# Layer 0's down-projection in three passes that mix context with halves of the latent blocks, and norm statistics by one product with a full matrix of 1/D

## The chip, the cores and the metric

The kernel runs on one core of a Trainium2 chip. The metric is the device time of one execution in microseconds (us); the time before is the median of three runs. The engines are PE (TensorE, matmuls), DVE (VectorE), ACT (ScalarE), POOL (GpSimd) and SP (SyncE), whose queue issues nearly all DMA transfers.

## The reference, cut to what matters

A diffusion transformer of two layers: 1024 latent tokens and 256 context tokens, width D = 1024. Each layer has a token mixer (differential attention in layer 0, neighbourhood attention in layer 1) and then a gated feed-forward network (FFN) of inner width 2816 with a short convolution over the positions. Latent and context share weights and are modulated by different vectors; layer 1 needs no context after its mixer.

```python
def rmsnorm(t, g):
    tf = tf * lax.rsqrt(jnp.mean(tf * tf, axis=-1, keepdims=True) + NORM_EPS)
    return tf * g
def conv_ffn(t, w_up, w_conv, b_conv, w_down):
    ...                                            # up-projection, depthwise conv of 3 taps
    return (jax.nn.silu(g) * a) @ w_down           # (n, 2816) @ (2816, 1024)
# in every layer, after the mixer:
    h2 = rmsnorm(x, norm_ffn[i]) * (1.0 + sc2) + sh2
    x = x + g2 * conv_ffn(h2, ...)
    if need_ctx:                                   # layer 0 alone
        xc = xc + cg2 * conv_ffn(hc2, ...)
```

The case is about the last product, `@ w_down`, and about the `mean` of the norm.

## The kernel before

**Layout and passes.** Activations lie with the features on the 128 partitions and the tokens along the free axis. There are three blocks of tokens: 0 and 1 (latent, 512 tokens each) and 2 (context, 256). The down-projection has 22 chunks k of the inner width and 8 chunks j of 128 output features. Every product runs as three matmuls of a high and a low part (high x high, high x low, low x high), so a block costs 22 x 8 x 3 = 528 matmuls of 512 columns, or 256 for the context. Layer 0 makes one pass for each block, in the order 2, 0, 1 (`ORDER`); layer 1 one for block 0 and one for block 1. A pass keeps its sums in eight PSUM banks, six from one pool and two from another. It takes k = 0 and 1 for six of the j, then k = 2, then the other two j, then k = 3 to 18 with all j, and at the end the last three k with j outside, so that the sums end one after the other; `end(j)` then combines a sum with x on DVE (L780), stores it (L782, layer 0) and adds its square to the norm's sums SS (L375 on ACT, L376 on DVE). For the context, x is loaded again just before that (L779), each into one of seven small buffers `t`; for blocks 0 and 1, x lies in a tile X that is loaded during the pass.

**The weights.** Each pass fetches all of `down` again: 22 tiles of 128x1024 (512 KB, L128), made into a high part on ACT (L138) and a low part on POOL (L142) in a ring `wsp` of five tiles, up to four ahead of PE.

**The activations g.** `load_g` brings the FFN's inner activations from DRAM into `t` (L758) and makes the high part on ACT (L555) and the low part on DVE (L556; the first four of a layer on POOL). They lie in two buffers of four k each, T1 and T2, used in turn and freed as a whole: a pass's first g can be written when the pass before has read its last g of that buffer.

**Work beside it in layer 0.** `hook0` adds work for layer 1. In pass 1 (block 0), after each k = 3 to 18, one of 16 quarters of layer 1's modulation weights is loaded into the one buffer `ug` (512 KB, L1238) and multiplied into `rows` by four DVE operations (L1244, L1246). At the start of pass 2 `ada_columns` (`turn`) turns `rows` into columns by 64 small matmuls (L1254) and frees the place where block 1's X goes. In pass 2 (block 1), after every other k = 3 to 17, a pair of up-projection tiles of layer 1 is loaded through the weights' raw buffers (two of four), added in four POOL operations (L182 to L185) and stored (two times 512 KB).

**The norm.** `rnorm_steps` makes 1/rms of a block for all partitions: for each 128 tokens a matmul of SS by a 128x2 matrix of 1/D (L388), which gives a column per 128 tokens; Sqrt (L391) and reciprocal (L392) of the columns; DVE spreads the columns on a diagonal (L394); a product with a matrix of ones brings them to all partitions (L398), and ACT copies the result to R (L399). The second product stands one section of PE's program later, where the generator is taken up again. The kernel calls it 13 times, 10 for 512 tokens and 3 for 256. In pass 2 of layer 0 it is called for block 0, whose norm for layer 1 (`write0`, 16 DVE operations, L412 and L414) follows there.

**The order.** PE's order in the FFN is that of the code (`manual(engines={pe})`); the other engines' orders are set by the scheduler. An engine's queue is served in order: what stands behind a waiting instruction waits too.

Of the kernel before, what the change touches and what calls it, by code (L numbers as in the profile page):

```python
# [52 lines left out]
ADA_AT = [(1, k) for k in range(3, 19)]  # L53
SUM_AT = [(2, k) for k in range(3, 19, 2)]
# [150 lines left out]
def _body(nc, tc, es, a, out):  # L205
# [58 lines left out]
    mean_w = const.tile([P, 2], F32, name="mean_w")  # L264
    V.memset(mean_w, 1.0 / D)
    ones = const.tile([P, P], F32, name="ones")
    V.memset(ones, 1.0)
    rcol, rn_count = const.tile([P, 2, 4], F32, name="rcol"), [0]
# [70 lines left out]
    def ada_dve(l, n, yp, pool, tag=None):  # L339
# [38 lines left out]
    def rnorm(*args):  # L378
        for R in rnorm_steps(*args):
            pass  # L380
        return R

    def rnorm_steps(yp, pool, SS, b0, n):

        nt = n // P
        ps = yp.tile([P, 512], F32, name="rn_ps", tag="y")
        for t in range(nt):
            T.matmul(out=ps[:, 2 * t:2 * t + 2], lhsT=SS[:, b0 + t * P:b0 + t * P + P], rhs=mean_w, start=True, stop=True)  # L388
        col = rcol[:, rn_count[0] % 2]
# [155 lines left out]
    def ffn(l, X, H, SS, np_, hp, hp2, xpool, yp, bp, hook=None, write=None, turn=None):  # L545
# [89 lines left out]
        with manual(engines={pe}):  # L635
            late, steps = [], None
            for i in range(NF if l == 0 else ne):
# [26 lines left out]
                if i == 1:  # L664
                    chain = rnorm_steps(yp, np_, SS, 512, 512)
                    next(chain)
                if i == 2:
                    R.append(next(chain))
                    steps = token_forms()
# [982 lines left out]
```

## Time and profile before

| | us |
|---|---|
| time, median of 3 runs | 3296.74 (3295.65 to 3296.87) |
| the profiled execution | 3302.75 |
| its span, first to last instruction | 3301.0 |
| PE busy | 3139.8 (95%) |
| DVE busy | 2141.8 (65%) |
| ACT busy | 1397.1 (42%) |
| POOL busy | 1750.4 (53%) |

The mean granted clock of PE is 0.971 of full speed. Layer 0's down-projection lies at 1566 to 1944 us of the span, that of layer 1 at 3036 to 3285. A stretch of the span is read by its busy times, by the count of its instructions in brackets, and by its granted clock (PEclk, 1.00 is full speed). An instruction's idle time in square brackets is that of its engine just before it, with the work that ended it.

### The profile page before, as it was taken

The page shows a single profiled execution, that of the slowest core. Times are in us where ns is not written, and L with a number is a line of the kernel's source. Part 1 is how long each engine was busy: PE and PEld are TensorE (multiplying, and loading weights), DVE is VectorE, ACT ScalarE, POOL GpSimd, SP SyncE. Part 2 cuts the span into 40 slices and gives each one's busy share as a digit, 9 for nine tenths or more (in the row PEclk, how much of TensorE's full clock was granted, in tenths as well). Part 3 has the DMA queues.
Part 4 walks back from the last instruction along what each step waited for, and adds up shares of the span by engine and source line. Part 5 has one row for each costly group of instructions (what it writes and reads, how often), then busy time and mean ns, then how long its engine had stood idle before and what let it go on. Part 6 is the DMA issues. An engine that isn't in the chain of part 4 may idle for free.

```text
span 3301.0 us, 43509 instructions
## 1 busy us (share of the span) xinstructions
PE 3139.8 (95%) x15632; PEld 2597.7 (79%) x15632; DVE 2141.8 (65%) x3294; ACT 1397.1 (42%) x2388; POOL 1750.4 (53%) x984
## 2 busy tenths in 40 slices
PE   8999889999899999999899989999999999999998
PEld 4888767777588888888777768888898778887876
DVE  6577488888547677777665554315995667776253
ACT  3221167777224454444332232225994444443111
POOL 2214166666227876777643752113663277777763
PEclk9999999999799999999998999999999999999999
DMA  7565334332525744344764667736884334334541
GB/s 265 158 205 185 121 104 119 105 111 70 191 95 193 232 159 141 131 144 154 237 219 172 216 234 252 244 131 167 194 206 145 100 126 144 130 122 159 199 166 58
DMA packets 248456, 536.82 MB, mean 163 GB/s; under 512 B 28976, under 2 KB 101552, under 8 KB 248240
## 3 DMA queue, kind: packets, MB, share of 16 engines
q1 hardware_dynamic: 247232, 533.71, 50.9%
q8 instruction: 124, 2.03, 0.3%
q14 instruction: 92, 0.75, 0.1%
q10 hardware_dynamic: 1008, 0.32, 0.0%
HBM read 395.24 MB, written 138.67 MB: 162 GB/s over the span
## 4 chain that ended last, share of the span: by engine, by line
PE 65%; DVE 11%; POOL 9%; issue 7%; DMA 5%; ACT 3%; SPq 0%; ACTq 0%; POOLq 0%; DVEq 0%
PE w_ps L609 21%; PE qk_ps L429 10%; PE w_ps L771 7%; POOL wsp L142 4%; PE wo_ps L429 3%; PE o L1048 3%; PE sl L997 2%; PE v_ps L440 2%; PE o L1438 2%; PE v_ps L439 2%; PE v_ps L441 2%; PE tp L1024 2%; PE w_ps L429 2%; DVE E L999 1%; POOL wf L150 1%
## 5 line engine op out<-in xcount | busy, mean ns | idle before, releaser
L142 POOL TENSOR_TENSOR wsp<-raw,wsp 128x1024 fp32r<-128x1024 f32 (+2 forms) x285 | 666.2, 2345 | 669.2 <-ACT wsp L138 570.4
L771 PE MATMUL w_ps<-g,wsp 128*128 128x512 f32 (+1 forms) x2640 | 568.6, 377 | 40.7 <-POOL wsp L142 14.6
L771 PEld LDWEIGHTS w_ps<-g,wsp 128*128 128x128 f32 x2640 | 471.4, 193 | 136.5 <-POOL wsp L142 17.8
L429 PE MATMUL qk_ps<-Hh,wsp 128*128 128x512 f32 x1280 | 319.7, 372 | 0.0
L140 POOL TENSOR_SCALAR wsp<-raw 128x1024 fp32r<-128x1024 f32 x72 | 100.2, 1393 | 391.9 <-DMA raw<-in_wqk_dram 150.0
L609 PE MATMUL w_ps<-FT,wf 128*128 128x512 f32 x1200 | 290.8, 394 | 12.2 <-ACT wf L149 5.8
L138 ACT CAST wsp<-raw 128x1024 fp32r<-128x1024 f32 (+1 forms) x213 | 193.8, 926 | 237.3 <-DMA raw<-in_down_dram 71.1
L609 PEld LDWEIGHTS w_ps<-FT,wf 128*128 128x128 f32 x1200 | 226.3, 189 | 64.9 <-POOL wf L150 6.6
L556 DVE TENSOR_TENSOR g<-t,g 128x512 fp32r<-128x512 f32 (+1 forms) x102 | 144.2, 1459 | 185.7 <-ACT g L555 183.1
L429 PEld LDWEIGHTS qk_ps<-Hh,wsp 128*128 128x128 f32 x1280 | 215.3, 188 | 38.2
L609 PE MATMUL w_ps<-FT,wsp 128*128 128x512 f32 x912 | 214.0, 390 | 0.0
L1004 ACT ACTIVATE E<-E,st 128x1280 f32<-128x1280 f32 x128 | 175.3, 1369 | 66.2 <-DVE st L999 65.1
L609 PEld LDWEIGHTS w_ps<-FT,wsp 128*128 128x128 f32 x912 | 171.1, 188 | 36.7 <-DVE t L700 0.2
L1014 POOL TENSOR_TENSOR E<-E,E 128x1280 f32<-128x1280 f32 x64 | 188.5, 2946 | 5.3
L1012 POOL TENSOR_SCALAR E<-E,st 128x1280 f32<-128x1280 f32 x64 | 85.9, 1342 | 191.9 <-DVE st L1007 103.4
L999 DVE CUSTOM_DVE_ANT_0 E<-sl,zero,st 128x1024 f32<-128x1024 f32 x128 | 163.7, 1280 | 21.4 <-PE sl L997 20.7
L429 PE MATMUL qk_ps<-Hl,wsp 128*128 128x512 f32 (+1 forms) x640 | 175.3, 371 | 0.0
L609 PE MATMUL w_ps<-Hh,wsp 128*128 128x512 f32 x528 | 173.7, 394 | 0.9 <-ACT p L621 0.9
L997 PE MATMUL sl<-kst,q 128*128 128x512 f32 x512 | 158.7, 433 | 1.6 <-DVE st L999 1.6
L353 DVE SCALAR_TENSOR_TENSOR ada<-raw,c_cvec,ada 128x512 f32<-128x512 f32 x168 | 135.5, 840 | 36.7 <-DMA raw<-in_ada_w_dram 35.4
L1048 PE MATMUL o<-T,vt 128*128 128x512 f32 (+1 forms) x464 | 154.2, 460 | 0.6 <-ACT ot L1055 0.5
L1375 POOL TENSOR_SCALAR E<-E,st 128x640 f32<-128x640 f32 (+1 forms) x128 | 99.5, 778 | 83.5 <-DVE st L1374 69.0
(608 smaller groups left out, 7024.1 us busy)
## 6 DMA issues: line engine op xcount, KB each, us to landing
raw<-in_down_dram SPq DMA_DIRECT2D x110, 512.0 KB
raw<-in_ada_w_dram SPq DMA_DIRECT2D x80, 512.0 KB
gscr<-work SPq DMA_DIRECT2D x44, 512.0 KB
t<-gscr SPq DMA_DIRECT2D x88, 256.0 KB
raw<-sscr SPq DMA_DIRECT2D x38, 512.0 KB
raw<-in_up_dram SPq DMA_DIRECT2D x33, 512.0 KB
raw<-in_wqk_dram SPq DMA_DIRECT2D x32, 512.0 KB
q<-qscr SPq DMA_DIRECT2D x256, 64.0 KB
```

Source lines behind the costliest of these rows:

```text
L138: nc.scalar.copy(out=sp[:, 0, c:c + n], in_=raw[:, c:c + n])
L142: nc.gpsimd.tensor_tensor(out=sp[:, 1, c:c + n], in0=raw[:, c:c + n], in1=f32(sp[:, 0, c:c + n]), op=ALU.subtract)
L353: stt(out=accs[v], in0=tv[:, kk, :], scalar=scol[:, kc, v:v + 1], in1=accs[v], op0=ALU.mult, op1=ALU.add)
L429: T.matmul(out=ps, lhsT=w[:, kc, :], rhs=H[b][s][:, kc, :], start=(kc == 0 and i == 0), stop=(kc == KC - 1 and i == 2))
L556: eng.tensor_tensor(out=form[:, kc, 1, :], in0=x, in1=f32(form[:, kc, 0, :]), op=ALU.subtract)
L609: T.matmul(out=ps, lhsT=w, rhs=form(kc, s), start=(start and kc + i == 0), stop=(kc == 3 and i == 2), skip_group_check=not start)
L771: T.matmul(out=ys[j][:, :n], lhsT=w[:, j, :], rhs=g[:, k % 4, s, :], start=(k == 0 and i == 0), stop=(k == NF - 1 and i == 2))
L997: T.matmul(out=ps[:, 512 * c:512 * c + 512], lhsT=qs[2 * j + s][:, qc], rhs=ks[j][:, 512 * c:512 * c + 512], start=(s == 0), stop=(s == 1))
L999: V.tensor_tensor_reduce(out=E[j][:, :SEQ], in0=ps, in1=zero.broadcast_to([P, SEQ]), op0=ALU.add, op1=ALU.min, scale=-1.0, scalar=m, accum ...
L1004: S.activation(out=E[j], in_=E[j], func=AF.Exp, scale=-1.0, bias=m, accum_out=sm)
L1014: G.tensor_tensor(out=E[0], in0=E[0], in1=E[1], op=ALU.add)
L1048: T.matmul(out=o[:, :n], lhsT=w, rhs=x, start=(i == 0 and j == 0), stop=(i == len(seq) - 1 and j == len(three) - 1))
```

## The change

**Passes.** `PASSES` gives each pass a list of segments (block, its j). Layer 0: pass 0 has the whole context and j = 0 to 3 of block 0; pass 1 has j = 4 to 7 of block 0 and j = 0 to 3 of block 1; pass 2 has j = 4 to 7 of block 1 and fetches only the right half of each weight tile (128x512). Two context sums share one PSUM bank. Layer 1 keeps its two passes. The count of matmuls is the same; the weight tiles of layer 0 become 44 whole and 22 half ones in place of 66, the g tiles 88 of 512 columns and 22 of 256 in place of 44 and 22.

**g.** Each of the two buffers is one ring whose slots are used again one by one. With two segments each has its ring, four k deep; with one segment both make a ring of eight. `load_g(at, k)` loads up to four (five) k ahead, over the end of the pass.

**Work beside it.** The modulation quarters move to pass 0, the sums of up weights to pass 1, `turn` stays at pass 1 (now the mixed pass), block 0's norm is made in pass 2 as before. A mixed pass keeps the last two k for the end, not three.

**Norm.** `rnorm` makes one product of a 128x128 matrix of 1/D with SS (128x512), which gives the mean on all partitions at once; Sqrt and reciprocal then work on 128x512, and there is no generator.

```diff
+ALL, LOW, HIGH = range(KC), range(4), range(4, KC)
+PASSES = ((((2, ALL), (0, LOW)), ((0, HIGH), (1, LOW)), ((1, HIGH),)), (((0, ALL),), ((1, ALL),)))
-ADA_AT = [(1, k) for k in range(3, 19)]
-SUM_AT = [(2, k) for k in range(3, 19, 2)]
+ADA_AT = [(0, k) for k in range(3, 19)]
+SUM_AT = [(1, k) for k in range(3, 19, 2)]
...
-    mean_w = const.tile([P, 2], F32, name="mean_w")
+    mean_w = const.tile([P, P], F32, name="mean_w")
...
-    def rnorm_steps(yp, pool, SS, b0, n):
...
+    def rnorm(yp, pool, SS, b0, n):
+        ps = yp.tile([P, 512], F32, name="rn_ps", tag="y")
+        T.matmul(out=ps[:, :n], lhsT=mean_w, rhs=SS[:, b0:b0 + n], start=True, stop=True)
+        R = pool.tile([P, 512], F32, name="R", bufs=rbufs[0])
+        S.activation(out=R[:, :n], in_=ps[:, :n], func=AF.Sqrt, bias=eps)
+        V.reciprocal(out=R[:, :n], in_=R[:, :n])
         return R
...
+        rings = hp2.tile([P, 4, 2, 512], F32R, name="g0", tag="T2"), hp.tile([P, 4, 2, 512], F32R, name="g1", tag="T1")
+        def slot(at, i, k):
+            q = at * NF + k
+            r = i if len(passes[at]) > 1 else q // 4 % 2
+            return rings[r][:, q % 4, :, :BLOCKS[passes[at][i][0]][1]].unsqueeze(1)
...
+            last = at * NF + k + (4 if len(passes[at]) > 1 else 5)
+            while loads and loads[0][0] * NF + loads[0][1] <= last:
...
+                        if b == 2 and j % 2:
+                            ys[i, j] = ys[i, j - 1][0], CTX
...
+                done = at > 0 and all(b for b, _ in segs)
+                if done:
+                    R.append(rnorm(yp, np_, SS, 0, 512))
...
+                if done:
+                    write(0, out_[0], R[-1])
...
+                n_last = 2 if len(segs) > 1 else 3
...
+                    load_g(at, k - 1)
...
+                    if item[1] < 2:
+                        end(item)
+                    elif x % 2:
+                        end(sums[x - 1])
+                        end(item)
...
+        for segs in PASSES[l]:
+            j0 = min(js[0] for _, js in segs)
             for k in range(NF):
-                W.add(a["down"][l, k])
+                W.add(a["down"][l, k][:, P * j0:])
```

**The order, first place: SP at the boundary between layer 0's passes 0 and 1.** `t<-xspill` loads x of one context chunk, `xscr<-t` stores its result, `xscr<-X` stores one of block 0, `raw` is a weight tile, `t<-gscr` a tile of g. Before:

```order
L782 DMA xscr<-t 128x256
L779 DMA t<-xspill_125 128x256
L128 DMA raw_14547<-in_down_dram 128x1024
L782 DMA xscr<-t 128x256
L779 DMA t<-xspill_125 128x256
L128 DMA raw_14597<-in_down_dram 128x1024
L128 DMA raw_14637<-in_down_dram 128x1024
L782 DMA xscr<-t 128x256
```

Now:

```order
L781 DMA xscr<-t 128x256
L778 DMA t<-xspill_124 128x256
L781 DMA xscr<-t 128x256
L778 DMA t<-xspill_124 128x256
L781 DMA xscr<-X_13805 128x512 x3
L781 DMA xscr<-t 128x256
L778 DMA t<-xspill_124 128x256
L781 DMA xscr<-X_13805 128x512
```

Three stores of block 0's ends now stand ahead of the load of x for the fifth context chunk; loads and stores of the context still take turns.

**Second place: DVE where the modulation rows are made.** `rows<-ug` is the work of L1246 (now L1253), four for a quarter, `g<-t,g` a low part of g. Before, in the block 0 pass:

```order
L1246 SCALAR_TENSOR_TENSOR rows<-ug,c_cvec,rows 128x512 x11
L556 TENSOR_TENSOR g_14995<-t,g_14995 128x512 x2
L1246 SCALAR_TENSOR_TENSOR rows<-ug,c_cvec,rows 128x512
L556 TENSOR_TENSOR g_14995<-t,g_14995 128x512 x2
L1244 TENSOR_SCALAR rows<-ug,c_cvec 128x512 x2
L1246 SCALAR_TENSOR_TENSOR rows<-ug,c_cvec,rows 128x512 x10
```

Now, in pass 0:

```order
L542 TENSOR_TENSOR g_13638<-t,g_13638 128x256
L1253 SCALAR_TENSOR_TENSOR rows<-ug,c_cvec,rows 128x512 x4
L542 TENSOR_TENSOR g_13639<-t,g_13639 128x512
L542 TENSOR_TENSOR g_13638<-t,g_13638 128x256
L1253 SCALAR_TENSOR_TENSOR rows<-ug,c_cvec,rows 128x512 x4
L542 TENSOR_TENSOR g_13639<-t,g_13639 128x512
```

One quarter now stands between the g of one k and that of the next.

**Third place: DVE at block 0's norm in layer 0's last pass.** L412 and L414 (now L398 and L400) are the norm's scaling and low part. Before:

```order
L392 RECIPROCAL rcol<-rcol 128x4
L394 TENSOR_TENSOR R<-c_ident,rcol 128x512
L556 TENSOR_TENSOR g_15384<-t,g_15384 128x512
L412 SCALAR_TENSOR_TENSOR X_14594<-X_14594,scale_1_93,R 128x512 x3
L414 SCALAR_TENSOR_TENSOR Hl_15509<-X_14594,mod_91,Hh_15508 128x512 x3
L412 SCALAR_TENSOR_TENSOR X_14594<-X_14594,scale_1_93,R 128x512 x4
L414 SCALAR_TENSOR_TENSOR Hl_15509<-X_14594,mod_91,Hh_15508 128x512 x4
L412 SCALAR_TENSOR_TENSOR X_14594<-X_14594,scale_1_93,R 128x512
L556 TENSOR_TENSOR g_15640<-t,g_15640 128x512 x2
```

Now:

```order
L385 RECIPROCAL R<-R 128x512
L542 TENSOR_TENSOR g_13638<-t,g_13638 128x512
L398 SCALAR_TENSOR_TENSOR X_13805<-X_13805,scale_1_92,R 128x512 x3
L400 SCALAR_TENSOR_TENSOR Hl_15968<-X_13805,mod_90,Hh_15967 128x512 x3
L398 SCALAR_TENSOR_TENSOR X_13805<-X_13805,scale_1_92,R 128x512 x4
L400 SCALAR_TENSOR_TENSOR Hl_15968<-X_13805,mod_90,Hh_15967 128x512 x4
L398 SCALAR_TENSOR_TENSOR X_13805<-X_13805,scale_1_92,R 128x512
L542 TENSOR_TENSOR g_13638<-t,g_13638 128x512 x2
```

The sequence is the same; the reciprocal is 128 times as wide for each partition, the spreading on the diagonal is gone, and the pass around it has four sums for each k in place of eight.

## Rows read from the trace of the kernel before

**Rows 1.** The page: span and engines (busy us, share of the span, instructions)
```profile
span 3301.0 us, 43509 instructions
...
PE 3139.8 (95%) x15632; PEld 2597.7 (79%) x15632; DVE 2141.8 (65%) x3294; ACT 1397.1 (42%) x2388; POOL 1750.4 (53%) x984
```

**Rows 2.** Six stretches of layer 0's down-projection; columns as named in the first line
```profile
core 0: us, PE busy (x) PEld busy (x) DVE busy (x) ACT busy (x) POOL busy (x), PEclk, DMA share, GB/s
1566.33:1640.65 74.32, 66.86 (x529) 65.24 (x527) 50.68 (x35) 29.51 (x42) 56.60 (x25) 0.95 0.72 239
1640.65:1674.61 33.96, 17.36 (x64) 13.11 (x63) 22.43 (x32) 7.40 (x13) 8.55 (x3) 0.80 0.56 174
1674.61:1796.83 122.22, 118.12 (x501) 95.92 (x502) 78.36 (x83) 42.79 (x57) 56.78 (x22) 0.97 0.63 216
1796.83:1809.00 12.17, 12.17 (x70) 12.17 (x68) 1.07 (x8) 0.00 (x0) 0.00 (x0) 0.60 0.00 1
1809.00:1881.30 72.30, 72.30 (x309) 58.88 (x309) 38.38 (x27) 22.13 (x30) 48.30 (x26) 0.97 0.61 221
1881.30:1944.42 63.12, 51.22 (x191) 39.63 (x191) 18.02 (x17) 15.19 (x21) 44.25 (x26) 0.86 0.74 259
```

**Rows 3.** Undisturbed context matmuls, then layer 1's two down passes; columns as in rows 2
```profile
1592.00:1602.00 10.00, 10.00 (x88) 10.00 (x87) 10.00 (x5) 4.07 (x6) 10.00 (x5) 1.00 0.74 232
3036.12:3156.20 120.08, 120.08 (x531) 99.27 (x529) 45.05 (x39) 19.34 (x31) 83.69 (x46) 1.00 0.55 185
3156.20:3284.60 128.40, 125.48 (x538) 102.50 (x537) 56.67 (x48) 23.44 (x39) 73.99 (x39) 0.97 0.36 119
```

**Rows 4.** PE in time, context pass to block 0: start, us, work [idle, releaser]
```profile
1649.41 0.79 PE L771 MATMUL w_ps<-g,wsp 128*128 128x512 f32 x1 [8.76 <-ACT g L555]
1655.33 8.73 PE L771 MATMUL w_ps<-g,wsp 128*128 128x512 f32 x29 [5.13 <-DVE g L556]
```

**Rows 5.** DVE in time, same boundary: first and last of the eight context ends
```profile
1637.49 0.47 DVE L780 SCALAR_TENSOR_TENSOR t<-w_ps,mod,t 128x256 f32<-128x256 f32 x1
...
1674.08 0.48 DVE L780 SCALAR_TENSOR_TENSOR t<-w_ps,mod,t 128x256 f32<-128x256 f32 x1
```

**Rows 6.** Modulation rows on DVE, 1698.76 to 1759.74 us: totals, then two quarters in time
```profile
L1246 DVE SCALAR_TENSOR_TENSOR rows<-ug,c_cvec,rows 128x512 f32<-128x512 f32 x28 | 24.8, 942 | 21.1 <-DMA ug<-in_ada_w_dram 21.1
...
L1244 DVE TENSOR_SCALAR rows<-ug,c_cvec 128x512 f32<-128x512 f32 x4 | 4.0, 1021 | 4.4 <-DMA ug<-in_ada_w_dram 4.3
...
1719.04 2.74 DVE L1246 SCALAR_TENSOR_TENSOR rows<-ug,c_cvec,rows 128x512 f32<-128x512 f32 x4 [2.91 <-DMA ug<-in_ada_w_dram]
1725.37 2.74 DVE L1246 SCALAR_TENSOR_TENSOR rows<-ug,c_cvec,rows 128x512 f32<-128x512 f32 x4 [3.58 <-DMA ug<-in_ada_w_dram]
```

**Rows 7.** The up-weight sums' first add on POOL: first and last of eight
```profile
L182 POOL TENSOR_TENSOR raw253g<-raw253g x1: 1738/1738/1738, 1829.1 to 1829.1; 128x512 f32<-128x512 f32 x1
...
L182 POOL TENSOR_TENSOR raw267g<-raw267g x1: 1277/1277/1277, 1929.3 to 1929.3; 128x512 f32<-128x512 f32 x1
```

**Rows 8.** Norm statistics and reciprocals, grouped by line and shape, whole span
```profile
L388 PE MATMUL rn_ps<-mean_w,SS 128*128 128x2 f32 x92 | 15.0, 283 | 11.1 <-DVE SS L376 11.1
...
L392 DVE RECIPROCAL rcol<-rcol 128x4 f32<-128x4 f32 x10 | 1.7, 174 | 11.6 <-ACT rcol L391 11.6
...
L1210 DVE RECIPROCAL m_all<-m_all 128x32 f32<-128x32 f32 x2 | 0.7, 352 | 0.8 <-ACT m_all L1209 0.8
```

**Rows 9.** DVE and POOL in time during block 0's norm in the block 1 pass
```profile
1821.13 10.26 DVE L412 SCALAR_TENSOR_TENSOR X<-X,scale,R 128x512 f32<-128x512 f32 x4
...
1821.00 8.15 POOL L142 TENSOR_TENSOR wsp<-raw,wsp 128x1024 fp32r<-128x1024 f32 x3 [32.03 <-ACT wsp L138]
```

**Rows 10.** DVE at the entry of layer 1's up-projection: its idle time and releaser
```profile
2613.70 8.79 DVE L565 SCALAR_TENSOR_TENSOR X<-X,scale,R 128x512 f32<-128x512 f32 x8 [8.56 <-ACT R L399]
```

**Rows 11.** The end of the kernel in time
```profile
3286.91 1.41 PE L388 MATMUL rn_ps<-mean_w,SS 128*128 128x2 f32 x8 [2.31 <-DVE SS L376]
...
3292.34 4.90 DVE L1527 TENSOR_TENSOR X<-X,R 128x512 f32<-128x512 f32 x8 [2.78 <-ACT R L399]
```

More of the change, by code (lines that the diff above doesn't have):

```diff
@@ L741, in ffn @@
                 fill()
[L744 to L745 removed]
+        passes, out_, need = PASSES[l], {}, {}
+        rings = hp2.tile([P, 4, 2, 512], F32R, name="g0", tag="T2"), hp.tile([P, 4, 2, 512], F32R, name="g1", tag="T1")
+        loads = deque((at, k) for at in range(len(passes)) for k in range(NF))
         W.scalar_high = l == 0
[L748 to L759 removed]
@@ new lines, in load_g @@
+        def load_g(at, k, eng=V):
+            last = at * NF + k + (4 if len(passes[at]) > 1 else 5)
+            while loads and loads[0][0] * NF + loads[0][1] <= last:
+                p, c = loads.popleft()
+                for i, (b, _) in enumerate(passes[p]):
+                    b0, w = BLOCKS[b]
+                    t = small()[:, :w]
+                    nc.sync.dma_start(out=t, in_=gscr[l][c][:, b0:b0 + w])
+                    split(slot(p, i, c), 0, t, eng)
+        load_g(0, -1, G)
@@ L785, in end @@
                         S.activation(out=x, in_=x, func=AF.Copy, scale=nout[:, j:j + 1])
+                early_ = sums[:len(sums) - n_late]
+                place(len(early_))
                 sps = [W.get() for _ in range(2)]
-                load_g(1)
-                for j in range(6):
+                load_g(at, -1)
+                for item in early_:
                     for k in range(2):
-                        down(k, j, sps[k])
-                if b == 1:
-                    if turn:
-                        turn()
-                    chain = rnorm_steps(yp, np_, SS, 0, 512)
-                    next(chain)
@@ new lines, in ffn @@
+                for item in sums[len(early_):]:
+                    for k in range(3):
+                        down(k, item, sps[k])
+                for b, _ in segs:
+                    if b < 2 and b not in out_:
+                        out_[b] = xpool.tile([P, KC, 512], F32, name=f"X{b}")
+                        for c in range(0, KC, 4):
+                            nc.sync.dma_start(out=out_[b][:, c:c + 4, :], in_=xspill[l][:, c:c + 4, 512 * b:512 * b + 512])
+                n_last = 2 if len(segs) > 1 else 3
@@ L824, in ffn @@
+                load_g(at, NF - n_last - 1)
+                for x, item in enumerate(sums):
+                    for k in range(n_last):
+                        down(NF - n_last + k, item, sps[k])
+                    if item[1] < 2:
[3 more added lines that the diff above has]
+                        end(item)
         return out_
```

107 lines of the change are left out of this document (32 added, 75 removed).

## The prediction

> **What bounds the kernel now.** I read the page first: of a span of 3301.0 us PE is busy 95% [rows 1], so time goes only where PE waits, runs at a low clock, or does work that can be dropped. The profiled execution took 3302.75 us, 1.75 beyond its span and 6.0 above the median of the three runs, 3296.74. I make the sum against the profiled execution and carry the difference over to the median.
>
> Next I cut layer 0's down-projection into six stretches [rows 2] and set each against the pace of undisturbed matmuls. 88 context records in 10.00 us make 0.114 us each, 531 of 512 columns in 120.08 us make 0.226 [rows 3]. 528 products of a pass should thus take 60.0 us for the context and 119.4 for a block: 298.8 in all, of 378.09 measured. The surplus by stretch [rows 2]:
> - Context pass: 74.32 - 60.0 = 14.3. POOL is busy 56.6 of the 74.3 us: a context pass eats a weight tile in 24 x 0.114 = 2.7 us, and POOL's subtract takes as long (three in 8.15 us, [rows 9]). Weight splitting limits it.
> - Boundary to block 0: 33.96 - 64 x 0.226 = 19.5. PE stands 8.76 us and 5.13 us for the new pass's g [rows 4], while the eight context ends crawl from 1637.49 to 1674.08 [rows 5], 36.6 / 7 = 5.2 us each: load x, combine, store, one after the other. Granted clock 0.80 there.
> - Block 0 to the modulation columns: 122.22 - 501 x 0.226 = 8.9, the next boundary with it.
> - The modulation columns: 12.17 us, in which 64 of the 70 records are the columns' small products; it stays, but for the norm's products in it (step 7).
> - First part of block 1: 72.30 - 309 x 0.226 = 2.4.
> - Its second part: 63.12 - 191 x 0.226 = 19.9. PE busy is 51.22, so 11.9 is waiting and 8.0 slow records at clock 0.86. Here POOL also makes the eight weight sums for layer 1, whose first adds are (1929.3 - 1829.1) / 7 = 14.3 us apart [rows 7], where PE needs two tiles in 48 x 0.226 = 10.9. Over eight sums PE should lose 8 x (14.3 - 10.9) = 27.6; 19.9 was lost, so the ring of split tiles covered 7.7.
> Surplus without the columns: 65.0 us.
>
> **The change part by part.** The products stay the same, 298.8 us. Weight loads fall (22 of the 66 tiles become halves), g loads and splits rise by 44 of 512 columns, 11.5 MB.
>
> 1. Start of pass 0. A weight tile now lasts 24 x 0.114 + 12 x 0.226 = 5.4 us against a POOL subtract of 2.7: the 14.3 goes. What is next late is g: POOL splits eight g tiles in place of four ahead of the pass. I leave 2 (0 to 8): -12.3.
>
> 2. Modulation rows in pass 0, one quarter between two pairs of g splits on DVE (order, second place). `ug` has one buffer, so a quarter is a load plus DVE's work. In the block 0 pass, 28 + 4 of these operations, eight quarters, took 60.98 us [rows 6]: 7.6 us each; undisturbed neighbours start 1725.37 - 1719.04 = 6.3 apart. A tile is wanted each 5.4 us and the splits stand four tiles ahead, 21.8 us. From the second quarter on there are 15 cycles: at 6.3 they lose 13, which the lead covers; at 7.6, 15 x 2.2 - 21.8 = 11. The splits fit into the wait for `ug` (2.91 and 3.58 us). I take 8 (0 to 20): +8.
>
> 3. Boundary 0 to 1. The g of k = 0 and 1 is now loaded early, since slots come free one by one; the two long waits for g go. The context ends stay serial, and the queue order (first place) puts three block 0 stores ahead of the loads for j = 4 to 7. From the last section's start the third block 0 end is at 8 x 0.68 + 3 x 1.36 = 9.5; four more loads and ends at 4.2 to 5.2 each end at 27 to 31. PE finishes its section at 10.9 and wants the last context bank three items later, at 15. So 12 to 16 us wait, less if pairs overlap, more at a low clock: 15 (8 to 20) for 19.5: -4.5.
>
> 4. Pass 1's other surplus. Its next boundary has no whole-tile wait and no serial ends: 5 (3 to 9) for 8.9: -3.9.
>
> 5. Sums in pass 1. They only move, and the pass carries two g loads for each tile. In two tiles the queue had as much as 7 transfers of 512 KB (two weights, two g of 256 KB, two loads and two stores of a sum: 3.67 MB); now as much as 8 (4.19 MB). At the late stretch's 259 GB/s [rows 2] these are 14.2 us, as measured, and 16.2. POOL's own work does not grow, and no norm burst runs beside it; I take 15.1: 8 x (15.1 - 10.9) - 7.7 = 26 (8 to 35) for 19.9: +6.1.
>
> 6. Block 0's norm in pass 2. That pass wants a tile each 12 x 0.226 = 2.7 us, half of before. The order (third place) has g of k = 6 behind nearly all 16 operations of the norm. R comes about 10.6 us into the pass (products of k = 0, 1, statistics, Sqrt, reciprocal), the operations take at least 16 x 0.7 = 11, and k = 6 is wanted at 17.3: 5 to 15 late, more under POOL [rows 9]. POOL's half tiles and the absence of sums shorten this. I take 8 plus 1 for the statistics, in place of 2.4: +6.6 (0 to +13).
>
> 7. Norms. The small products L388 go: 92 records, 15.0 us of PE [rows 8]; the wide product that replaces L398 has its size. Some ran in PE's idle time, so I count two thirds: -10 (-15 to 0). The reciprocal grows from 4 to 512 elements. The trace has 174 ns for 4 and 352 for 32 [rows 8], 6.4 ns an element, so 3.4 us by that slope; at least the 0.7 of a plain operation, and the slope may not hold. DVE is busy 65% [rows 1]; its cover is gone only in step 6 and at the end, where the chain from L388 to the first scaling took 3286.91 to 3292.34, 5.4 us [rows 11], and the new one takes a product (1 to 2), Sqrt (0.6) and 3.4: about 0.
> [...]
>
> 8. Layer 1. At its up-projection's entry DVE idles 8.56 us until R [rows 10], whose second product stood late in PE's order; that step is gone: -2 (0 to -4), as PE has queued work there. The second down pass took 128.40 against 119.4 [rows 3]; without the whole-tile wait -3 (0 to -6).
>
> Sum: -12.3 + 8 - 4.5 - 3.9 + 6.1 + 6.6 = 0.0 for the down-projection, -10 and -5 beside it: -15. Profiled 3287.8; median 3281.7, say 3282.
>
> **The rivals.** *The DMA share decides (no change).* Pass 1's cycle is the full 16.2: 35 in step 5 instead of 26, 3282 + 9 = 3291. For: 259 GB/s at a DMA share of 0.74 while PE waited. Against: other stretches have shares of 0.6 with spare time.
>
> *DVE paces pass 0 (slower).* Where POOL splits without pause DVE slows: four operations took 10.26 us beside three POOL subtracts of 8.15 [rows 9]. If each quarter catches one such subtract, its cycle is 6.3 + 2.7 = 9.0, with a g split behind it 9.7: losses of 15 x 3.6 - 21.8 = 32 to 15 x 4.3 - 21.8 = 43 instead of 8: 3306 to 3317, say 3311. It turns the sign when the cycle passes 5.4 + (23 + 21.8) / 15 = 8.4 us. Against: POOL is only half busy in the mixed pass, and 7.6 was measured with POOL splitting a tile each 5.5 us.
> [...]
>
> *The losses of the sums are mostly covered (larger gain).* With no burst before them and a full ring, the 14.3 cycle loses only 12, and the context ends overlap in pairs (8): -14 and -7, 3261. Against: step 5's extra bytes.
>
> *The passes don't overlap as written* would show as whole-tile waits at boundaries; the order rules it out.
>
> **How the numbers follow.** Forecast 0.46 (3282, its own range 3270 to 3296), larger gain 0.16, no change 0.20, slower 0.18. All low ends together lie 54 below the forecast, all high ends 57 above; independent steps do not all fall on one side, so I take a little under half of each: 3258 to 3308. What this kernel's measurement can tell from no change is 0.2%, 6.6 us. Faster: 0.85 of the forecast, all of the larger gain, a sixth of the no-change case: 0.58; within 0.2%: 0.23; slower: 0.19.
>
> **What would show it.** Right: pass 0 about 131 us with no POOL wait at its start; one stop of 10 to 15 us before pass 1's fourth item; sums 15 us apart and PE waits of POOL late in pass 1; a stop at k = 6 of pass 2; no small products; RECIPROCAL of 128x512 near 3.4 us. Wrong: `rows` more than 8.4 us apart, reciprocals of 5 us or more, or sums that PE does not feel.

## The result, and the profile after

The changed kernel took 3313.31 us (median of 4 runs, 3308.07 to 3328.21) against 3296.8 before: a ratio of 1.0055, 95% interval 1.0039 to 1.0072. It is slower, by more than the 0.2% that the prediction had set as a bound, and above the predicted range. The profiled execution took 3314.94 us with a span of 3313.2, 12.2 more than that of before.

Single executions scatter: 25 of the kernel before lie between 3288.7 and 3304.6 us, ten of e3 (below) between 3292.2 and 3316.0. Part of it may arise in the last third of layer 0's up-projection, where PE makes 177 or 178 matmuls in 40 us in the profiles of before and of the changed kernel, among others, and 164 to 168 in those of e1, e4, e5, e8 and e10. So I compare profiles stage by stage, and whole times by their ratio.

The first fence shows the changed kernel in six stretches, to be read against [rows 2] and [rows 3]: pass 0, the boundary with pass 1's first products, the modulation columns, the rest of pass 1, pass 2, and layer 1's two down passes. Columns as in [rows 2].

```profile
1569.54:1711.50 141.96, 129.51 (x793) 116.00 (x791) 93.23 (x110) 45.87 (x71) 68.98 (x29) 0.96 0.65 222
1711.50:1738.61 27.11, 12.89 (x38) 9.13 (x37) 13.14 (x24) 7.40 (x14) 4.93 (x2) 0.84 0.56 170
1738.61:1752.12 13.51, 13.51 (x66) 13.51 (x64) 1.35 (x5) 2.47 (x4) 0.00 (x0) 0.50 0.19 68
1752.12:1895.00 142.88, 124.32 (x494) 97.26 (x495) 69.11 (x53) 41.82 (x62) 94.52 (x52) 0.93 0.72 264
1895.00:1972.00 77.00, 66.98 (x269) 53.46 (x269) 49.12 (x53) 36.90 (x61) 31.18 (x22) 0.91 0.60 192
3056.54:3296.95 240.41, 240.41 (x1059) 198.42 (x1057) 100.30 (x82) 43.61 (x67) 162.42 (x85) 1.00 0.46 156
```

The down-projection of layer 0 takes 1569.54 to 1972.0, 402.5 us, where it took 378.1. Layer 1's takes 240.41 where it took 120.08 + 128.40 = 248.5: PE is busy from end to end at clock 1.00, and the whole-tile wait is gone. The remaining 4.1 of the gain is spread over the other stages (layer 0's down-projection starts 3.2 later, and what lies between and behind the two is 7.3 shorter). So +24.4 - 8.1 - 4.1 = +12.2, the difference of the spans.

Where PE stood in pass 0 (first its waits in all: us, times, the longest, then the two longest), in the boundary and in pass 2 (PE in time: start, us, work, idle before it and what ended it):

```profile
PE w_ps L768 <- DVE g L542: 10.8, 6, 4.3
PE w_ps L768 <- POOL g L542: 1.7, 1, 1.7
...
1684.39 10.43 PE L768 MATMUL w_ps<-g,wsp 128*128 128x512 f32 x51 [3.20 <-DVE g L542]
1699.08 12.45 PE L768 MATMUL w_ps<-g,wsp 128*128 128x256 f32 x68 [4.26 <-DVE g L542]
...
1714.20 1.63 PE L768 MATMUL w_ps<-g,wsp 128*128 128x512 f32 x6 [2.68 <-DVE t L779]
1719.43 5.97 PE L768 MATMUL w_ps<-g,wsp 128*128 128x512 f32 x18 [3.60 <-DVE X L779]
1730.16 2.93 PE L768 MATMUL w_ps<-g,wsp 128*128 128x512 f32 x6 [4.76 <-DVE t L779]
1736.27 2.54 PE L768 MATMUL w_ps<-g,wsp 128*128 128x512 f32 x6 [3.18 <-DVE t L779]
...
1903.34 0.50 PE L768 MATMUL w_ps<-g,wsp 128*128 128x512 f32 x1 [2.01 <-ACT g L541]
...
1925.09 46.90 PE L768 MATMUL w_ps<-g,wsp 128*128 128x512 f32 x191 [7.78 <-DVE g L542]
```

In pass 0 PE waited for low parts of g, and just behind the two longest waits the granted clock was 0.50 (1686 to 1688 us) and 0.54 (1699.08 to 1701). The boundary that answers to [rows 4] has no wait for g any more; its waits are for context ends (`t`, L779) and a block 0 end, 14.2 us in four pieces. The last row is the wait for g of k = 6 behind the norm.

DVE in pass 0, from its start to the second quarter of the modulation rows, then two of the last three quarters; below it POOL beside the five splits:

```profile
1578.19 4.60 DVE L617 SCALAR_TENSOR_TENSOR work<-uh,c_ffn_conv,work 128x512 f32<-128x512 f32 x2
1582.90 1.58 DVE L717 TENSOR_TENSOR work<-work 128x1024 f32<-128x1024 f32 x1
1588.50 0.89 DVE L1251 TENSOR_SCALAR rows<-ug,c_cvec 128x512 f32<-128x512 f32 x2 [4.02 <-DMA gscr<-work]
...
1596.01 11.40 DVE L542 TENSOR_TENSOR g<-t,g 128x512 fp32r<-128x512 f32 x5 [2.94 <-ACT g L541]
1607.32 2.73 DVE L1253 SCALAR_TENSOR_TENSOR rows<-ug,c_cvec,rows 128x512 f32<-128x512 f32 x4
...
1693.86 4.82 DVE L1253 SCALAR_TENSOR_TENSOR rows<-ug,c_cvec,rows 128x512 f32<-128x512 f32 x4 [3.16 <-DMA ug<-in_ada_w_dram]
...
1709.33 2.74 DVE L1253 SCALAR_TENSOR_TENSOR rows<-ug,c_cvec,rows 128x512 f32<-128x512 f32 x4 [2.71 <-DMA ug<-in_ada_w_dram]
```

```profile
1593.70 13.41 POOL L144 TENSOR_TENSOR wsp<-raw,wsp 128x1024 fp32r<-128x1024 f32 x5 [8.07 <-ACT wsp L140]
```

Fifteen quarters start from 1607.32 to 1709.33, (1709.33 - 1607.32) / 14 = 7.3 us apart; [rows 6] gave 7.6 and 6.3. DVE reached the second quarter 37.8 us after pass 0's start: it was still at the convolution of the up-projection until 1584, waited for a store of it, and made five g splits in 11.40 us while POOL made five of its own in 13.41; four of the five took 2.6 to 2.9 us, in place of 0.69 for 512 columns and 0.42 for 256.

The norm's new instructions, grouped by line and shape, with the columns of [rows 8]:

```profile
L385 DVE RECIPROCAL R<-R 128x512 f32<-128x512 f32 x10 | 33.5, 3348 | 10.9 <-ACT R L384 10.8
L385 DVE RECIPROCAL R<-R 128x256 f32<-128x256 f32 x3 | 5.2, 1744 | 0.2 <-ACT R L384 0.2
...
L382 PE MATMUL rn_ps<-SS,mean_w 128*128 128x512 f32 (+1 forms) x26 | 13.8, 615 | 7.0 <-DVE SS L377 7.0
```

The 92 small products (15.0 us) are gone, the wide one takes what L398 took, and a reciprocal of 512 elements takes 3.35 us, the 3.4 of the slope.

### The profile page after: what moved, and what is told of

Its sections match the earlier page's. It is cut to its first block, busy times and chain, and to the rows that moved or that the text cites. A ratio compares the mean times of both kernels' runs of the same rounds, so it can differ in the third digit from the quotient of the medians.

```text
span 3313.2 us, 43614 instructions
## 1 busy us (share of the span) xinstructions
PE 3134.2 (95%) x15540; PEld 2589.3 (78%) x15540; DVE 2173.2 (66%) x3320; ACT 1411.9 (43%) x2419; POOL 1740.7 (53%) x989
## 4 chain that ended last, share of the span: by engine, by line
PE 61%; POOL 11%; DVE 10%; issue 8%; DMA 7%; ACT 3%; SPq 1%; POOLq 0%; DVEq 0%; ACTq 0%
PE w_ps L595 20%; PE qk_ps L415 9%; PE w_ps L768 8%; POOL wsp L144 3%; PE o L1054 3%; PE sl L1003 2%; PE v_ps L427 2%; PE v_ps L425 2%; PE v_ps L426 2%; POOL wf L152 2%; PE o L1445 2%; PE wo_ps L415 2%; PE tp L1030 2%; PE w_ps L415 2%; DVE E L1005 1%
## 5 line engine op out<-in xcount | busy, mean ns | idle before, releaser
L144 POOL TENSOR_TENSOR wsp<-raw,wsp 128x1024 fp32r<-128x1024 f32 (+2 forms) x285 | 647.7, 2277 | 718.4 <-ACT wsp L140 581.8
L140 ACT CAST wsp<-raw 128x1024 fp32r<-128x1024 f32 (+2 forms) x213 | 184.8, 881 | 233.0 <-DMA raw<-in_down_dram 71.9
L542 DVE TENSOR_TENSOR g<-t,g 128x512 fp32r<-128x512 f32 (+1 forms) x141 | 166.5, 1216 | 169.2 <-ACT g L541 163.1
L541 ACT CAST g<-t 128x512 fp32r<-128x512 f32 (+1 forms) x154 | 87.5, 588 | 219.0 <-DMA t<-gscr 115.3
```

What stands on the lines that cost most here:

```text
L140: nc.scalar.copy(out=sp[:, 0, c:c + n], in_=raw[:, c:c + n])
L144: nc.gpsimd.tensor_tensor(out=sp[:, 1, c:c + n], in0=raw[:, c:c + n], in1=f32(sp[:, 0, c:c + n]), op=ALU.subtract)
L542: eng.tensor_tensor(out=form[:, kc, 1, :], in0=x, in1=f32(form[:, kc, 0, :]), op=ALU.subtract)
```

## The experiments

All durations of a stage are those of the one profiled execution of a kernel, from its first to its last product; ratios are to the kernel before on the same chip. How far a single stage can be trusted: in the seven profiles that leave pass 0 and its boundary as the change made them, or nearly (the changed kernel, e2, e4, e7, e8, e9, e11), pass 0 took 133.9 to 149.3 us, four of them 141.8 to 142.2, and pass 0 and boundary together 164.9 to 179.1.

**The norm alone and the passes alone.** The first kernel is that of before with the new `rnorm`, the second the changed kernel with the old `rnorm_steps` and its two places in PE's program:

```diff
# e1: kernel before
...
-                    chain = rnorm_steps(yp, np_, SS, 0, 512)
-                    next(chain)
+                    R.append(rnorm(yp, np_, SS, 0, 512))
...
# e2: changed kernel
-                    R.append(rnorm(yp, np_, SS, 0, 512))
+                    chain = rnorm_steps(yp, np_, SS, 0, 512)
+                    next(chain)
...
```

> The kernel before with the new norm alone (one product with the full matrix, wide Sqrt and reciprocal), passes unchanged. Theory A (the mixed passes lose the time, the norm gains a little): outside layer 0's down-projection the changed kernel was 12 us shorter than the kernel before, of which 8 us lie in layer 1's down-projection, where the g ring is new too. So the norm alone gains 4 to 10 us: 3287 to 3293, 128x512 reciprocals of 3.35 us. Rival B (the wide reciprocal is what costs the time): slower than 3300.

> The changed kernel with the old norm (small products, diagonal, second product one section later). Theory A: the passes alone cost what the changed kernel lost and the norm's gain on top: 3317 to 3323. Rival B (the reciprocal in the last pass and at the entries costs): 3300 or below.

Measured: the norm alone 0.9995 (0.9981 to 1.0009), the passes alone 1.0062 (1.0044 to 1.0080). The passes make the kernel slower; e2's 3319.2 us are what Theory A gave. The norm changes next to nothing: e1's 3297.7 lie between its two theories. It gains in the up-projection of layer 1 (462.4 us before and 460.8 in e2, but 456.6 in e1 and 458.0 in the changed kernel, from the first norm product to the first down product), and part of that is paid back at the kernel's start. There layer 0's first norms stand ahead of the first query products. These products by line (least, median and greatest duration in ns, then the first and the last start in us), in the changed kernel:

```profile
L415 PE MATMUL qk_ps<-Hh,wsp x768: 278/390/476, 116.1 to 353.7; 128*128 128x512 f32 x128, 128*128 128x256 f32 x64
```

and in e2:

```profile
L431 PE MATMUL qk_ps<-Hh,wsp x768: 278/390/629, 107.3 to 347.7; 128*128 128x512 f32 x128, 128*128 128x256 f32 x64
```

The kernel before starts them at 110.7 and e1 at 115.0: both kernels with the wide reciprocal come 4 to 5 us later than the kernel before, e2 does not. In both, PE stands 4.74 us for the first normalised activations (`Hh`), in e2 0.24. In e1's profile layer 0's down-projection is 10.1 us shorter too (368.0 for 378.1), but its up-projection is one of those with 165 to 167 matmuls in 40 us; in how many executions the one makes up for the other is not known. In layer 1's down-projection e1 takes 245.7 and e2 241.4: of the 8.1 us gained there, 7 come from the ring for g.

**Mixing undone, the rest kept.** The changed kernel with whole blocks as passes:

```diff
-PASSES = ((((2, ALL), (0, LOW)), ((0, HIGH), (1, LOW)), ((1, HIGH),)), (((0, ALL),), ((1, ALL),)))
+PASSES = ((((2, ALL),), ((0, ALL),), ((1, ALL),)), (((0, ALL),), ((1, ALL),)))
-ADA_AT = [(0, k) for k in range(3, 19)]
+ADA_AT = [(1, k) for k in range(3, 19)]
-SUM_AT = [(1, k) for k in range(3, 19, 2)]
+SUM_AT = [(2, k) for k in range(3, 19, 2)]
...
-                if turn and at == 1:
+                if turn and at == 2:
```

> The changed kernel with its rings for g and its norm, but layer 0 in the old passes (context, block 0, block 1, whole weight tiles), modulation quarters and sums where the kernel before has them. Theory A (mixing the blocks in one pass is what costs: twice the g loads beside the quarters and the sums): the down-projection of layer 0 falls from 402 us to 365 to 375, the whole to 3275 to 3290. Rival E (the rings or the norm burst cost, not the mixing): the down-projection stays over 390, 3300 or more.

Measured: 0.9996 (0.9981 to 1.0010); the down-projection of layer 0 takes 379.8 us, 22.7 less than mixed. That settles the side: the mixing costs. The whole time is not shorter than before, though, where Theory A had 3275 to 3290, and the stage missed Theory A's 365 to 375, because with a ring the context's ends still hold up the next pass, here longer than before (columns as in [rows 2], context pass and boundary):

```profile
1584.70:1654.60 69.90, 66.48 (x530) 65.75 (x529) 51.83 (x34) 29.51 (x43) 58.02 (x25) 0.95 0.68 230
1654.60:1695.10 40.50, 12.71 (x37) 8.31 (x35) 22.89 (x31) 6.75 (x12) 7.85 (x3) 0.67 0.59 193
```

40.5 us for 36 products (8.1): 32 us lost.

**Pass 0: the one buffer `ug`.** Odd quarters go to two tiles that are idle there:

```diff
-        t = np_.tile([P, 1024], F32, name="ug")
-        nc.sync.dma_start(out=t, in_=a["ada_w"][1, n, k])
+        src = a["ada_w"][1, n, k]
+        if k % 2:
+            t = [np_.tile([P, 512], F32, name="p1", bufs=NP1[0]) for _ in range(2)]
+            for kk in range(2):
+                nc.sync.dma_start(out=t[kk], in_=src[:, 512 * kk:512 * kk + 512])
...
```

> The changed kernel, but odd quarters of the modulation weights are loaded into two idle half tiles, so that a quarter's load no longer waits for DVE's work on the quarter before. Theory A (the one buffer makes a quarter last 7.3 us in pass 0 where PE wants a tile each 5.4, and PE waits 14 us for g behind it): pass 0 falls from 142 to about 128 us, the time to 3297 to 3302. Rival C (DVE itself is late, held up by POOL's splits): pass 0 keeps 138 us or more, 3310 to 3315.

Measured: 3310.21 us, 1.0034 (1.0016 to 1.0051), its profiled execution one of its two fastest (3292.32; the other eight took 3306.7 to 3316.0). Pass 0, the boundary and the columns:

```profile
1569.46:1701.90 132.44, 126.97 (x794) 113.58 (x793) 111.51 (x120) 48.48 (x77) 70.97 (x30) 0.99 0.73 245
1701.90:1719.50 17.60, 11.17 (x37) 8.13 (x37) 8.88 (x14) 5.02 (x10) 4.96 (x2) 0.73 0.63 198
1719.50:1730.00 10.50, 10.50 (x66) 10.50 (x64) 1.05 (x4) 2.47 (x4) 0.00 (x0) 0.66 0.20 71
```

Pass 0 falls by 9.5 us, between the two forecasts, and PE's waits for DVE's g in it from 10.8 to 3.4. The boundary behind it falls by 9.5 more, since DVE now comes to the first context end 9.7 us ahead of the pass's end (1692.2) and not 1.1 behind it (1712.6). Pass 0 and boundary together take 150.0 us, 14.9 below the least of the seven above, and e10 repeats it (pass 0 in 133.4 us). So the wait for the one buffer is shown to cost in both places; but of pass 0's 22.3 us of loss, 132.4 - 119.7 = 12.7 are left: 5.5 of waits (3.4 for DVE's g, 1.8 for POOL's) and 7.3 of slower products. The whole time did not follow: its median lies where Rival C had it, 3 us below the changed kernel's (7 by the ratios), and only two of ten executions show the 22 us of this profile. Why is not known.

**The boundary: serial loads of x.** First the loads were put on ACT's queue; then x was loaded in pairs of chunks into idle tiles, two pairs ahead of the last section:

```diff
# e4
-                        nc.sync.dma_start(out=x, in_=xspill[l][:, j, b0:b0 + n])
+                        nc.scalar.dma_start(out=x, in_=xspill[l][:, j, b0:b0 + n])
# e6
-                        x = small()[:, :n]
-                        nc.sync.dma_start(out=x, in_=xspill[l][:, j, b0:b0 + n])
+                        x = xc[j // 2][:, j % 2, :]
...
+            xc[c] = np_.tile([P, 2, CTX], F32, name="p1", bufs=NP1[0])
+            nc.sync.dma_start(out=xc[c], in_=xspill[l][:, 2 * c:2 * c + 2, SEQ:])
```

> The changed kernel, but the loads of x for the context ends are issued by ACT's queue, so they no longer stand behind the stores of earlier ends on SP's. Theory A (the boundary of passes 0 and 1 is lost to the serial loads): its 19 us fall to 8 or less, 3300 to 3305. Rival D (the ends are late because of DVE, or because the seven small buffers are taken by g): the boundary keeps 15 us or more, 3309 to 3315.

> The changed kernel, but x of the context ends is loaded in pairs of chunks into two idle tiles, the first two pairs before the last section. Theory A (serial loads of x through the ring of small buffers): the stretch between the end of pass 0 and the modulation columns falls from 27.1 to 10 to 16 us (8.1 are products). Rival D (DVE's or ACT's order keeps the ends late): it stays over 22.

Measured: on ACT's queue the boundary grew from 27.1 to 33.9 us, and the kernel took 3324.52 us, 1.0072 (1.0052 to 1.0091); its pass 0 was shorter by as much, 133.9, so that the two together took 167.8 for 169.1. In pairs the boundary fell to 16.7, just beside Theory A's 10 to 16, with pass 0 at 141.5 (one run, 3318.58). On ACT's queue the loads were no less serial (ACT in time):

```profile
1729.49 0.42 ACT L376 ACTIVATE sq<-t 128x256 f32<-128x256 f32 x1 [0.64 <-DVE t L779]
1729.57 0.33 ACTq L778 DMA_DIRECT2D t<-xspill  x1
1734.29 0.42 ACT L376 ACTIVATE sq<-t 128x256 f32<-128x256 f32 x1 [4.38 <-DVE t L779]
1734.37 0.33 ACTq L778 DMA_DIRECT2D t<-xspill  x1
```

Each load now stands behind the square of the end before it, which waits for DVE. So e4 did not test what it was meant to; e6 did, and the serial loads are shown to hold 10 of the boundary's 19 us. The other half hangs on the late quarters that e3 removes; with both edits (e10) nothing is left of it.

**Pass 2: the norm ahead of g.** POOL makes the low parts of g in that pass:

```diff
-                    split(slot(p, i, c), 0, t, eng)
+                    split(slot(p, i, c), 0, t, G if p == 2 else eng)
```

> The changed kernel, but in pass 2 POOL makes the low parts of g in place of DVE, so that they no longer stand behind the norm of block 0. Theory A (the norm's 16 operations and the reciprocal hold up g of k = 6, and that is the loss of pass 2): pass 2 falls from 77 us to 64 to 68. Rival F (pass 2 is held up by loads or the clock): it stays at 74 or more.

Measured: 71.7 us in place of 77.0 (one run, 3314.73). That lies between the two forecasts. The wait for k = 6 is gone, but PE then waits 3.4 us for g of k = 2 and shortly for weights at k = 11 and 12 (0.2 to 1.0 us), now that POOL splits both. The norm is part of the loss (5.3 us here), not all of it.

**Pass 1: what sets the cycle of the sums.** Three kernels: stores of the sums on POOL's queue, half of the sums in idle tiles, and one g load for both splits of a k.

```diff
# e8
-            self.nc.sync.dma_start(out=dst[:, 1024 * k:1024 * k + 1024], in_=t)
+            self.nc.gpsimd.dma_start(out=dst[:, 1024 * k:1024 * k + 1024], in_=t)
# e9, odd pairs i
+            ra = np_.tile([P, 1024], F32, name="ug")
+            nc.sync.dma_start(out=ra, in_=a["up"][1, i])
+            rg = [np_.tile([P, 512], F32, name="p1", bufs=NP1[0]) for _ in range(2)]
...
# e11
-                    t = small()[:, :w]
-                    nc.sync.dma_start(out=t, in_=gscr[l][c][:, b0:b0 + w])
+                    if not (l == 0 and p == 1 and i == 1):
...
```

> The changed kernel, but the sums of up weights are stored by POOL's queue, so that SP's queue does not wait for POOL's adds ahead of the next loads of g and weights. Theory A (in pass 1 PE waits for g whose load stood in SP's queue behind such a store): from the end of the columns to the end of pass 1 142.7 us falls to 120 to 130. Rival B (the DMA rate or the two raw buffers set the cycle of 15.3 us): it stays over 137.

> The changed kernel, but every other pair of up-projection tiles for the sums is loaded into tiles that are idle in pass 1, not into two of the four raw buffers that the weights need. Theory G (the four raw buffers set the cycle of 15.3 us per two tiles): from the end of the columns to the end of pass 1 142.7 us falls to 125 to 132. Rival B (the rate of the DMA engines sets it: 4.19 MB in 15.3 us, 274 GB/s): it stays over 137.

> The changed kernel, but in pass 1 block 1's g is not loaded: both splits of a k read block 0's g, so the loads of a tile fall from 4.19 to 3.67 MB per two tiles while weights, raw buffers, splits and sums stay (block 1's result is thus wrong). Rival B (the rate of the DMA engines sets pass 1's cycle): the sums come 13.5 to 14 us apart in place of 15.5, and from the columns to the end of pass 1 142.7 us falls to 128 to 134. Theory G (the chain load, adds, store in the two raw buffers sets it): 15 us and more apart, 138 or more.

The three took 3344.74, 3319.06 and 3319.64 us (one run each). Of e8's 31 us above the changed kernel, 24 lie ahead of layer 0's down-projection, where its edit moves the stores of other sums too and its up-projection has the slower rhythm. The first adds of the sums on POOL, first and last of the changed kernel, then of e11:

```profile
L184 POOL TENSOR_TENSOR raw231g<-raw231g x1: 1747/1747/1747, 1770.9 to 1770.9; 128x512 f32<-128x512 f32 x1
...
L184 POOL TENSOR_TENSOR raw245g<-raw245g x1: 1487/1487/1487, 1879.3 to 1879.3; 128x512 f32<-128x512 f32 x1
```

```profile
L184 POOL TENSOR_TENSOR raw231g<-raw231g x1: 1734/1734/1734, 1772.6 to 1772.6; 128x512 f32<-128x512 f32 x1
...
L184 POOL TENSOR_TENSOR raw245g<-raw245g x1: 1260/1260/1260, 1880.7 to 1880.7; 128x512 f32<-128x512 f32 x1
```

(1879.3 - 1770.9) / 7 = 15.5 us in the changed kernel and (1880.7 - 1772.6) / 7 = 15.4 in e11, though e11 moves 227 GB/s there in place of 264. So the rate of the DMA engines does not set the cycle, and the forecast's step 5, which took it from the bytes, was right in size (15.1) for a wrong reason. With the stores on POOL's queue the stretch stayed at 143.4, but PE's wait moved: in the changed kernel it was for g (first two rows: us, times, the longest), in e8 mostly for POOL's weights (last row) and 6.6 us for g:

```profile
PE w_ps L768 <- DVE g L542: 10.8, 7, 2.0
PE w_ps L768 <- ACT g L541: 7.7, 4, 2.3
...
PE w_ps L768 <- POOL wsp L144: 13.8, 5, 7.1
```

In e9, while only even pairs ran, PE kept its pace (columns as in [rows 2]; the first stretch up to the first odd pair's adds, then the rest of pass 1, then pass 2):

```profile
1765.50:1857.40 91.90, 91.25 (x384) 73.53 (x384) 48.42 (x36) 28.84 (x41) 60.08 (x30) 0.97 0.69 249
1857.40:1895.80 38.40, 30.24 (x108) 22.61 (x108) 13.90 (x11) 11.41 (x17) 22.78 (x14) 0.87 0.76 267
1895.80:1977.60 81.80, 66.28 (x269) 52.72 (x270) 51.81 (x59) 39.27 (x64) 30.89 (x22) 0.92 0.59 186
```

384 products in 91.9 us are 5 more than at full pace, and the stretch falls from 142.9 to 130.3, as Theory G had it. But the odd pairs came late and partly fell into pass 2, which grew to 81.8, so this shows only that fewer sums at a time cost less. e10 below has the same edit, and there all eight sums ran in pass 1 (its first and its last add, then the stretch):

```profile
1756.69 1.75 POOL L184 TENSOR_TENSOR raw231g<-raw231g 128x512 f32<-128x512 f32 x1
...
1867.85 1.70 POOL L184 TENSOR_TENSOR p<-p,p 128x512 f32<-128x512 f32 x1 [0.58 <-DMA p<-in_up_dram]
...
1739.40:1883.80 144.40, 125.87 (x494) 98.20 (x494) 66.19 (x52) 41.66 (x61) 95.78 (x54) 0.92 0.72 258
```

(1867.85 - 1756.69) / 7 = 15.9 us, with only every other pair in the raw buffers. So the chain through two of the four raw buffers (load, four adds, store, next load) does not set the cycle alone either, and Theory G fails as e8's Theory A did. What fits them all is that either is enough, inferred and not shown: e8 takes the stores out of SP's queue and leaves the raw buffers, e9 and e10 relieve the buffers and leave the stores ahead of the loads of g. No run takes both away, and the cause of the cycle stays open. The kernel before had one of the same kind: [rows 7] had 14.3.

**All of it together, and the old passes with what was learnt.** e10 joins e3, e6, e7 and e9; e12 is e5 with the pairs of e6.

> The changed kernel with the edits that remove a named wait: modulation quarters into two places in turn, x of the context in pairs, low parts of g on POOL in pass 2, every other sum in idle tiles. If the losses are separate, the down-projection of layer 0 falls from 402 us by 22 (quarters, with the boundary behind them), 5 to 10 (x in pairs, part of it the same stretch), 5 (pass 2) and, if the raw buffers matter, 10 to 15: 355 to 368, the time 3266 to 3282. If DMA sets pass 1's pace: 368 to 376, 3282 to 3290. If the waits only move on (Rival C): over 390, 3300 or more.

> The changed kernel's rings and norm with the old three passes (as e5), and x of the context in pairs. Theory A (mixing costs more than it saves; the boundary of the context pass is lost to the serial loads of x and the g loads behind them): the down-projection of layer 0 falls from e5's 380 to 350 to 360 us, and the time to 3275 to 3285, below the kernel before and below e10. Rival D (the boundary's wait moves on to the g loads or the weights): 370 or more, 3292 to 3300.

Measured: e10 takes 3295.14 us, 0.9987 (0.9977 to 0.9996), with 370.6 us for the down-projection, 31.9 less than the changed kernel; e12 takes 3281.11, 0.9953 (0.9936 to 0.9971), with 362.4. e10's stage is that of its second forecast (pass 1 as slow as it was, though not for the DMA's sake, by e11), its time above it; e12's time is as forecast, its stage 2.4 above. So the mixed passes can be brought to a hair below the kernel before, and the unmixed ones with the ring, the new norm and paired loads of x are below it by 0.3 to 0.6%, and below the changed kernel by about 1%. e10's pass 0, boundary and pass 2 (columns as in [rows 2]):

```profile
1585.20:1718.60 133.40, 126.49 (x794) 113.44 (x793) 114.14 (x120) 46.95 (x74) 68.42 (x29) 0.99 0.74 246
1718.60:1726.80 8.20, 8.20 (x39) 6.68 (x37) 5.81 (x9) 4.37 (x8) 3.21 (x2) 1.00 0.64 224
...
1883.80:1955.80 72.00, 65.84 (x269) 51.85 (x269) 38.44 (x28) 35.52 (x60) 60.97 (x42) 0.95 0.60 194
```

Its boundary is free of waits at a clock of 1.00; pass 0 and boundary together take 141.6 us. e12's context pass and its boundary, then the block 0 pass:

```profile
1572.90:1644.50 71.60, 65.80 (x530) 64.60 (x529) 61.27 (x35) 30.00 (x44) 60.67 (x26) 0.98 0.68 232
1644.50:1666.50 22.00, 10.36 (x38) 6.96 (x36) 15.38 (x24) 6.63 (x13) 8.24 (x3) 0.82 0.71 239
1666.50:1790.10 123.60, 123.60 (x528) 101.16 (x529) 73.34 (x85) 39.06 (x51) 58.76 (x22) 0.98 0.57 200
```

The boundary falls from e5's 40.5 to 22.0, and the block 0 pass runs with all the quarters in it and without one wait: PE is busy in all of its 123.60 us. There DVE has one g split a k beside a quarter, and two in the mixed pass.

## Why the prediction was wrong

The surplus over 298.8 us of products, stage by stage, as predicted and as measured (each stretch above less its products at 0.114 and 0.226 us):

| term | predicted | measured |
|---|---|---|
| pass 0: start and quarters (steps 1, 2) | 2 + 8 | 142.0 - 119.7 = 22.3 |
| boundary 0 to 1 (step 3) | 15 | 27.1 - 36 x 0.226 = 19.0 |
| modulation columns | 12.2, less the norm's products | 13.5 |
| rest of pass 1 (steps 4, 5) | 5 + 26 | 142.9 - 492 x 0.226 = 31.7 |
| pass 2 (step 6) | 9 | 77.0 - 59.7 = 17.3 |
| layer 0's down-projection against before | 0 | +24.4 |
| norms (step 7) | -10 | about -2 (ratios of e1, and of e2 against the changed kernel) |
| layer 1's down boundary and entry (step 8) | -5 | -8.1 in the down-projection |

- **Step 1 held.** PE never waits for POOL's weights in pass 0 or at its start, but for one wait of 1.7 us for a g split by POOL. Of the 14.3 us that the context pass lost before, though, only 7.5 were waits (74.32 - 66.86 in [rows 2]); the rest were slower products, and those came back (step 2).
- **Step 2 failed, the largest miss.** The cycle of a quarter was right, 7.3 us for a forecast between 6.3 and 7.6. The lead was not: "the splits stand four tiles ahead, 21.8 us" holds for PE's program, but DVE came to the second quarter 37.8 us into the pass, with k = 4 to 6 and half of k = 7 split, and PE, 224 matmuls into the pass, was at k = 6 itself. With no lead PE goes at DVE's pace. Of the 22.3 us lost, 12.5 are waits, 10.8 of them for low parts of g, and 9.8 are slower products, at a mean clock of 0.96. I had read where the splits stand in the order and not when DVE gets there: the rows before pass 0 (the convolution's tail, the store) were not in the working. The slower rival had this place and came near the measured time (3306 to 3317), yet by a cycle of 9 or more that did not occur; its break-even of 8.4 us was wrong for the same reason. This step alone did not turn the sign: with a second buffer (e3) the kernel is still slower than before, 1.0034.
- **Step 3 was near in size, with half of it from elsewhere.** The waits are 14.2 us (forecast 12 to 16), in four stops and not one. e6 confirms the serial loads, for 10 of the 19.0 us; the rest came from step 2, whose last quarter stands ahead of the first context end on DVE (e3). The clock took more than I had: granted 0.84 in the boundary and 0.50 in the columns behind it, where the kernel before had 0.60.
- **Steps 4 and 5 were right in sum (31.7 for 31) by luck.** The sums came 15.5 us apart for 15.1, but not for their bytes (e11), and PE did not wait for POOL's weights late in pass 1, as the signs had it, but 18.5 us for g. What sets the cycle stays open.
- **Step 6 was right in place** (7.78 us for g of k = 6) and short by 8: I counted that wait, not the second one (2.01 us) and a mean clock of 0.91 in the pass.
- **Step 7 failed on where the reciprocal is uncovered.** Of the 10 us about 2 came, not told from none. The reciprocal's 3.35 us were as worked out, but "only in step 6 and at the end" left out the start, where 4 to 5 us are lost.
- **Step 8 was right in its direction,** and larger: 8.1 in the down passes for 3.

None of the signs of being wrong came: `rows` were 7.3 us apart, the reciprocal took 3.35, and PE felt the sums. Of the rivals, the DMA share is refuted (e11), the larger gain did not come, and DVE was slowed beside POOL most in one place: five splits in 11.40 us beside five of POOL's in 13.41. At their undisturbed 0.69 and 0.42 the five would have taken 2.9 us, so some 8.5 of the lead went there; in the cycles it showed in single quarters only (4.82 us for four operations that take 2.74 elsewhere).

## What to carry to other kernels

A lead that stands in the order of instructions is worth only what the engine has when the stage begins (here DVE came to the second quarter 37.8 us into the pass): follow the engine that keeps the lead back through the stage before. A pass that carries twice the inputs for each step leaves less room beside it on DVE for side work that was sized for one (with all quarters beside it DVE was busy 111.5 of 132.4 us in e3's pass 0, and 73.3 of 123.6 in e12's block 0 pass); price the side work by its cycle (one buffer: load plus use, here 7.3 us) against the step (5.4), and give it a second buffer before mixing (here 9.5 us in the pass and as much in the boundary behind it, in the profile). A wait for which one queue and one ring of buffers are each enough does not yield to an edit of either (inferred here from pass 1 behind the columns: 142.9 us, 143.4 in e8, 144.4 in e10). And a part of a change that gains in one place (here the rings, 7 us in layer 1) can be kept without the part that loses.

## What the runs showed of the hardware that was not expected

A reciprocal on DVE took 3.35 us for 512 elements of a partition's row and 1.74 for 256, (3.348 - 1.744) / 256 = 6.3 ns for each further element, where the short ones had 6.4 (174 ns for 4 and 352 for 32, [rows 8]). Stops of PE were followed by slow products: behind the four of the boundary, 14.2 us in all, the 64 small products of the modulation columns ran at a granted clock of 0.50 throughout and took 13.5 us. In e5 PE had been busy without a break for 122.8 us ahead of them, with a clock of 1.00 in the 100 us of the first row; there the clock fell in the modulation columns themselves, to a mean of 0.71 (columns as in [rows 2]), and they took 9.8. That the stops made it fall lower is inferred from this difference:

```profile
1700.00:1800.00 100.00, 100.00 (x439) 82.22 (x438) 57.96 (x61) 29.36 (x37) 51.69 (x19) 1.00 0.54 185
...
1817.83:1827.60 9.77, 9.77 (x66) 9.77 (x64) 2.44 (x6) 3.44 (x5) 0.00 (x0) 0.71 0.37 142
```

And the up-projection before all this has two rhythms, 177 or some 166 matmuls in 40 us at the same granted clock of 1.00, in the profiles of different kernels that share its code; whether one kernel has both, and what sets them, was not looked into.
